# Bidirectional retention: from all 512 x 512 scores to two chunks of 256 tokens with states

## The chip, the cores and the metric

One core of a Trainium2 chip runs the whole program. The metric is device time in microseconds (us): the median of the runs, 1824.52 us before (3 runs, 1824.33 to 1824.80).

## The reference, cut to what matters

Two sequences ("groups") of 512 tokens and 1024 features go through two layers and a final norm. Layer 0 is differential attention, layer 1 is retention in both directions over 8 heads, with 128 features in queries and keys and 256 in values. The change lies in layer 1.

```python
proj = h @ w_in                                # 1024 -> q 1024, k 1024, v 2048, gate 2048
q, k = retention_rotate(q), retention_rotate(k) * 128 ** -0.5
# per head, with decays g_f = exp(log_g_f), g_b = exp(log_g_b); n: query, m: key
# forward:  o_f[n] = sum over m <= n of g_f ** (n - m) * (q[n] . k[m]) * v[m]
# backward: o_b[n] = sum over m >  n of g_b ** (m - n) * (q[n] . k[m]) * v[m]
o = rms_norm(o_f + o_b) * silu(gate)
x = x + o @ w_out
```

The reference takes the sums in chunks of 128 tokens with a state of 128 x 256 carried between them; any other chunk gives the same sums.

## The kernel before, in words

**Numbers in two parts.** Each fp32 operand of a matmul is held as a rounded part (`hi_of`, L469, a cast on ScalarE) and the rest (`lo_of`, L472, a subtraction on VectorE; its instructions stand under L470 and L473). A product takes three passes: hi*hi, hi*lo, lo*hi (`PASSES`, L31).

**Stages.** Projections of layer 0, attention (about 620 to 1000 us), projections of layer 1 (about 1050 to 1500 us), retention with its output projection (1480 us to the end). The projections and the output projections multiply 2 x 2 blocks in seven products (`SEQ`, L44; matmuls L645, L693 and L1384). Rotated queries and keys (`rot_done`, L741), values and gates go to DRAM and come back for the next stage.

**Retention before.** A block is one head and one group: 16 blocks, ordered by pairs of heads (two heads of group 0, the same two of group 1). For a block, `fetch2` (L1549) loads the two parts of q and of k (512 KB each, [128 features, 2, 512 tokens]) and of v (2 x 512 KB), `decay` (L1568) a table of 128 x 896 decays for each head. `score2` (L1572) works on 128 keys and all 512 queries: three matmuls of 512 columns, one multiplication with the table from PSUM on VectorE (L1583), then hi and lo. Four such steps make the block's transposed scores. `av2` (L1589) makes the output of 128 queries: 12 matmuls of 256 columns (4 tiles of keys x 3 passes, L1597). Then the norm (`norm_two` L864, `norm_apply` L885: a square with a sum, a root, a reciprocal, a scaled copy, L868 to L887), two transposes back into the same PSUM bank (`turn_o` L890, matmuls L893), the gate (`gate2` L1318, L1326), sums for the seven products (L1344 to L1358), and `out2` (L1360, L1384), 28 calls of six matmuls of 512 columns for each pair of heads. The weights of a pair are loaded in seven pieces of 512 KB by `w_split` (L1303) into two buffers in turn (`wa`, `wb`) and split by ScalarE and VectorE (1024 columns each). They are due between the last `out2` of one pair and the first of the next.

**The order of the work.** The main loop (L1632 to L1659) walks over 64 tiles (block b, 128 queries t): while tile t of block b is in `av2`, step t of block b+1 is in `score2`, and pieces of `out2` (`fill`) stand between. At t = 3 `fetch2(b + 2)` is called. Nothing is issued there: each call notes operations with a cost, what they read and write, and `Plan.arrange` (L141) simulates the five engines and writes one fixed order for each. PE may be moved by up to 24 operations (`WINDOW`, L75), a load is issued up to 15 us of planned time ahead (`AHEAD`, L79). An engine then takes its list strictly in order and waits at each semaphore.

**Places.** `LATE` (L374) names the buffers of the retention stage; two sets serve even and odd blocks. PSUM: two banks `sc` for scores, two banks `o` for `av2` with its norm and transposes, four for `out2`. The decay tables are made in the projection stage (`decay_table`, L1512: three exponentials a head, L1524 to L1526) and go through DRAM.

## Time and profile before

| what | us |
|---|---|
| median of 3 runs | 1824.52 |
| the profiled execution, own time | 1824.4 |
| its span, first to last instruction | 1822.6 |
| PE (matmuls) busy | 1784.9 (98%) |
| PEld (weight loads, beside PE) busy | 1539.8 (84%) |
| DVE (VectorE) busy | 1477.9 (81%) |
| ACT (ScalarE) busy | 1037.9 (57%) |

The profile is one execution. "Busy" is the time with at least one instruction of that engine under way; since matmuls are pipelined, the time that a matmul costs is read from the distance between starts, not from its own duration. The chain is followed back from the last instruction: each piece is what the next one waited for.

### The profile page before, as it was taken

The numbers are of one execution on the slowest core, as the hardware profiler recorded it, in microseconds if no ns is written. First come the engines' busy times: TensorE is split into PE (matmuls) and PEld (weight loads), VectorE is DVE, ScalarE is ACT, GpSimd is POOL, SyncE is SP. The second block draws the span as 40 slices with busy tenths as digits, with TensorE's granted clock in tenths as the row PEclk, the third lists the DMA queues.
The fourth block names the chain that finished last, engine by engine and source line by source line (L and its number), as shares of the span: only waits on it lengthen the run. The fifth ranks groups of instructions, "written<-read, shape, count | busy, mean of one in ns | idle before, by whom it ended". The sixth has DMA issues, their size and how long they took to land.

```text
span 1822.6 us, 28127 instructions
## 1 busy us (share of the span) xinstructions
PE 1784.9 (98%) x10106; PEld 1539.8 (84%) x10106; DVE 1477.9 (81%) x2599; ACT 1037.9 (57%) x2158; POOL 238.4 (13%) x371
## 2 busy tenths in 40 slices
PE   7999999999999989999999999999999999999998
PEld 6988988988988878888888788989898897888886
DVE  7988888787798799888888898786766858778687
ACT  7644444444444587767767774544453547666564
POOL 3000000000000024343433100000000000111111
PEclk9999999999999999999999999999999999999999
DMA  8467667767766678888786358788775478889784
GB/s 290 164 184 199 201 188 201 207 184 209 197 182 193 229 288 226 238 233 249 230 249 188 135 168 235 233 233 236 228 220 161 151 255 296 247 239 268 221 248 139
DMA packets 197421, 393.85 MB, mean 216 GB/s; under 512 B 16289, under 2 KB 77345, under 8 KB 197153
## 3 DMA queue, kind: packets, MB, share of 16 engines
q1 hardware_dynamic: 174320, 349.76, 57.7%
q0 software_dynamic: 22528, 41.95, 14.3%
q8 instruction: 79, 1.29, 0.3%
q14 instruction: 62, 0.50, 0.1%
q10 hardware_dynamic: 432, 0.34, 0.1%
HBM read 254.10 MB, written 175.64 MB: 236 GB/s over the span
## 4 chain that ended last, share of the span: by engine, by line
PE 82%; DMA 7%; DVE 6%; ACT 2%; issue 2%; POOL 1%; SPq 0%; ACTq 0%; DVEq 0%; POOLq 0%
PE bank L645 39%; PE bank L693 16%; PE bank L1384 12%; PE bank L1267 4%; PE bank L1217 4%; DMA b<-w1P 4%; PE bank L1597 3%; DMA b<-in_da_w_out_dram 1%; PE bank L1579 1%; PE bank L1252 1%; DVE b L473 1%; PE bank L893 1%; DVE arena L473 1%; ACT arena L470 1%; DMA raw<-in_ret_w_in_dram 1%
## 5 line engine op out<-in xcount | busy, mean ns | idle before, releaser
L645 PE MATMUL bank<-arena,ws 128*128 128x512 f32 x2202 | 526.8, 393 | 7.9 <-ACT ws L470 7.0
L645 PEld LDWEIGHTS bank<-arena,ws 128*128 128x128 f32 x2202 | 414.0, 189 | 98.4 <-ACT ws L470 7.0
L645 PE MATMUL bank<-b,ws 128*128 128x512 f32 x1170 | 286.7, 392 | 1.3 <-DVE e L722 1.3
L645 PEld LDWEIGHTS bank<-b,ws 128*128 128x128 f32 x1170 | 219.2, 188 | 48.9 <-DVE e L722 1.4
L1384 PE MATMUL bank<-b,b 128*128 128x512 f32 x794 | 212.3, 399 | 2.8 <-ACT c L1423 1.8
L693 PE MATMUL bank<-ws,arena 128*128 128x256 f32 x1728 | 205.4, 277 | 1.7 <-DVE e L794 1.7
L470 ACT CAST ws<-st 128x512 fp32r<-128x512 f32 (+1 forms) x188 | 129.8, 694 | 132.2 <-PE bank L645 64.0
L693 PEld LDWEIGHTS bank<-ws,arena 128*128 128x128 f32 x1728 | 201.9, 188 | 3.1 <-DVE e L794 1.9
L714 ACT COPY c<-bank 128x512 f32<-128x512 f32 x165 | 96.4, 585 | 166.7 <-PE bank L645 134.1
L473 DVE TENSOR_TENSOR ws<-st,ws 128x512 fp32r<-128x512 f32 (+1 forms) x188 | 144.8, 775 | 50.7 <-ACT ws L470 43.4
L1384 PEld LDWEIGHTS bank<-b,b 128*128 128x128 f32 x794 | 144.8, 189 | 32.9 <-ACT c L1423 2.3
L473 DVE TENSOR_TENSOR b<-b,b 128x512 fp32r<-128x512 f32 (+2 forms) x204 | 137.0, 683 | 22.7 <-ACT b L470 22.4
L470 ACT CAST b<-b 128x512 fp32r<-128x512 f32 (+2 forms) x204 | 123.7, 620 | 44.0 <-DVE b L1583 16.3
L722 DVE TENSOR_TENSOR e<-bank,c 128x512 f32<-128x512 f32 x165 | 113.0, 685 | 40.7 <-PE bank L645 32.1
L473 DVE TENSOR_TENSOR ws<-raw,ws 128x512 fp32r<-128x512 f32 (+1 forms) x143 | 109.5, 773 | 34.7 <-ACT ws L470 20.6
L960 POOL DMA_DIRECT2D x<-b x96 | 85.9, 908 | 365.1 <-DVE b L1428 265.1
L470 ACT CAST ws<-raw 128x512 fp32r<-128x512 f32 (+1 forms) x143 | 99.0, 698 | 51.7 <-PE bank L645 33.0
L693 PE MATMUL bank<-ws,b 128*128 128x256 f32 x960 | 117.7, 277 | 0.0
L693 PEld LDWEIGHTS bank<-ws,b 128*128 128x128 f32 x960 | 114.0, 188 | 0.9
L1233 ACT ACTIVATE b<-bank,nm 128x512 f32<-128x512 f32 x128 | 87.8, 688 | 36.7 <-DVE nm L1225 36.2
L1267 PE MATMUL bank<-arena 128*128 128x256 f32 x768 | 105.7, 287 | 0.2 <-DVE b L1326 0.2
L1217 PE MATMUL bank<-arena 128*128 128x512 f32 x384 | 102.1, 398 | 3.4 <-ACT b L1233 3.4
(190 smaller groups left out, 2812.8 us busy)
## 6 DMA issues: line engine op xcount, KB each, us to landing
qk<-os SPq DMA_DIRECT2D x192, 256.0 KB, 3.9
arena<-qk SPq DMA_DIRECT2D x80, 512.0 KB, 6.2
raw<-in_da_w_in_dram SPq DMA_DIRECT2D x64, 512.0 KB, 5.8
v<-os SPq DMA_DIRECT2D x60, 512.0 KB, 5.3
arena<-v SPq DMA_DIRECT2D x48, 512.0 KB, 5.2
x<-b POOLq DMA_DIRECT2D x96, 256.0 KB, 6.5
raw<-in_ret_w_in_dram SPq DMA_DIRECT2D x48, 512.0 KB, 5.9
g<-e SPq DMA_DIRECT2D x49, 256.0 KB, 5.6
```

The source lines that it names most:

```text
L470: act(n, lambda: nc.scalar.copy(dst(), src()), r, w)
L473: dve(n, lambda: nc.vector.tensor_tensor(dst(), src(), hi().bitcast(F32), op=ALU.subtract), r, w)
L645: nc.tensor.matmul(ps.t, a[u][0]()[:, k, :], bt[k][:, v, :], start=(opens and k == 0 and i == 0), stop=(k == 3 and i == 2), skip_group_che ...
L693: nc.tensor.matmul(ps[:, (t % 2) * 256:(t % 2) * 256 + 256], bt[k][:, v, t * P:(t + 1) * P], a[u][0]()[:, k, :], start=(opens and t % 2 == ...
L714: act(S, lambda c=c, ps=ps: nc.scalar.copy(c.t, ps.t), [ps], [c])
L722: dve(S, lambda e=e, ps=ps, c=c: nc.vector.tensor_tensor(e.t, ps.t, c.t, op=ALU.add), [ps, c], [e])
L960: plan.op("POOL", 1.0, lambda: nc.gpsimd.dma_start(out(), in_(), accum_op=ALU.add), r, w, lands=5.5, kb=kb, hold=hold)
L1217: nc.tensor.matmul(s.t, q[:, u, t * P:(t + 1) * P], k[:, v, :], start=(n == 0), stop=(n == 2))
L1233: act(840, lambda j=j, s=s, m=m: nc.scalar.activation(p[:, j, :], s.t, AF.Exp, bias=m.t, accum_out=sm[:, j:j + 1]), [s, m], [(p, j), (sm, j)])
L1267: nc.tensor.matmul(o[:, 0:256], aT[:, a, j * P:(j + 1) * P], v[b][:, j, :], start=(n == 0), stop=(n == 11))
L1384: nc.tensor.matmul(ps.t, pick(A[i], u), (hi, lo)[v][:, i, :], start=(opens and n == 0), stop=(n == 5), skip_group_check=True)
L1597: nc.tensor.matmul(o[:, 0:256], a_[j][:, u, t * P:(t + 1) * P], v_[v][:, j, :], start=(n == 0), stop=(n == 11))
```

## The change

Retention is computed in two chunks of 256 tokens. Scores are made only inside a chunk (`score2(b, c)`: two tiles of keys x 256 queries, side by side in one bank). Across chunks a state carries the sum: `states` multiplies the transposed, decay-scaled keys of each chunk with its values (128 x 256 for each chunk, one bank), and `av2` adds the decay-scaled queries (`queries`) times the state of the other chunk, which serves forward for chunk 1 and backward for chunk 0. Keys are stored once in fp32 (256 KB a block instead of 512); `keys` splits them on chip, transposes them by TensorE (four transposes into one bank), scales each transposed tile by a column of decays on the way out of PSUM (four copies of 128 columns on ScalarE) and splits the result. The decay tables of a head, 512 KB instead of 448, are one 128 x 512 table for scores, which fits both chunks, one for queries, and four columns for keys. The steps of block b+1 beside tile t of block b are now `keys`, `score2` of chunk 0, `states` with `queries`, `score2` of chunk 1. The fp32 keys have one place for all blocks, and transposed keys and scaled queries share one place in each set. The kernel's other stages keep their code.

```diff
...
-    LATE = dict(q0=["raw0"], k0=["raw1"], v0=["raw2", "raw3"], aT0=["st0", "st1", "st2", "os0"], sg0=["os1"], F0=[3],
-                aT1=[0, 1, 2, "os2"], k1=[4], q1=[5], v1=[6, 7], AB=[8, 9, 10], sg1=[26], F1=[27], wa=[20], wb=[21], S4=[24],
+    LATE = dict(q0=["raw0"], k0=["raw1"], v0=["raw2", "raw3"], aT0=["st0", "st1"], kT0=["st2"], Z0=["os0"], sg0=["os1"], F0=[3],
+                aT1=[0, 1], kT1=[2], Z1=["os2"], k1=[4], q1=[5], v1=[6, 7], AB=[8, 9, 10], sg1=[26], F1=[27], wa=[20], wb=[21], S4=[24],
...
@@ rot_done @@
+            if whole:
+                o = os_t(F32)
+                for n, (p, q, alu) in enumerate(((m1, m2, ALU.subtract), (a, m3, ALU.add))):
+                    dve(S, lambda n=n, p=p, q=q, alu=alu: nc.vector.tensor_tensor(o[:, n, :], p.t, q.t, op=alu),
+                        [p, q], [(o, n)])
+                    for j in range(2):
+                        dma(lambda j=j, n=n: dst[g][j, n * 64:(n + 1) * 64], lambda j=j, n=n: o[j * 64:(j + 1) * 64, n, :],
+                            [(o, n)], [(dst[g], (n, j))], 128)
+                return
...
-    f_d = [dram([P, 896], f"f{h}") for h in range(NH)]
+                        shape = [2, P, S] if layer and which else [2, P, 2, S]
+                        qk_d[layer, which, h, g] = dram(shape, f"qk{layer}{which}{h}{g}")
+    f_d = [dram([P, 2, S], f"f{h}") for h in range(NH)]
     x_d = {(g, t): dram([P, D], f"x{g}{t}") for g in range(NG) for t in range(NT)}
...
@@ decay_table @@
-        act(384, lambda: nc.scalar.activation(a[:, 0:384], a[:, 0:384], AF.Exp, scale=lr[:, 1, h:h + 1]), [lr], [a])
-        act(384, lambda: nc.scalar.activation(b[:, P:S], b[:, P:S], AF.Exp, scale=lr[:, 0, h:h + 1]), [lr], [b])
-        act(P, lambda: nc.scalar.activation(b[:, 0:P], mid.t, AF.Exp), [mid], [b])
-        dma(lambda: f_d[h][:, 0:384], lambda: a[:, 0:384], [a], [(f_d[h], 0)], 192)
-        dma(lambda: f_d[h][:, 384:896], lambda: b.t, [b], [(f_d[h], 1)], 256)
-
+        for n, which in ((0, 1), (3, 0)):
+            at = slice(n * P, n * P + P)
+            act(P, lambda at=at, which=which: nc.scalar.activation(
+                f[:, at], f[:, at], AF.Exp, scale=lr[:, which, h:h + 1]), [lr], [f])
+        for n in (1, 2):
+            act(P, lambda n=n: nc.scalar.activation(f[:, n * P:n * P + P], mid.t, AF.Exp), [mid], [f])
+        for which in range(2):
+            at, half = slice(which * 2, which * 2 + 2), slice((1 - which) * 256, (2 - which) * 256)
+            act(60, lambda at=at, which=which: nc.scalar.activation(
+                dtab[:, h, at], cols[:, at], AF.Exp, scale=lr[:, which, h:h + 1]), [lr, cols], [(dtab, 2 * h + which)])
+            act(256, lambda half=half, which=which: nc.scalar.activation(
+                w[:, half], w[:, half], AF.Exp, scale=lr[:, which, h:h + 1]), [lr], [w])
+        for n, x in enumerate((f, w)):
+            dma(lambda n=n: f_d[h][:, n, :], lambda x=x: x.t, [x], [(f_d[h], n)], 256)
...
@@ fetch2 @@
-        for which in range(2):
-            t = qk[b, which] = late("qk"[which] + str(b % 2), 0, [P, 2, S], F32R)
-            src = qk_d[1, which, h - h % 2, g]
-            dma(lambda t=t: t.t.bitcast(F32), lambda src=src: src[h % 2], [src], [t], 512)
+        q = qk[b, 0] = late("q" + str(b % 2), 0, [P, 2, S], F32R)
+        q_src, k_src = (qk_d[1, which, h - h % 2, g] for which in range(2))
+        kf = kfs[b] = Buf(plan, "kf", 1, lambda i: small[:, 512:1024], lambda i: (-512, 0))
+        dma(lambda: kf.t, lambda: k_src[h % 2], [k_src], [kf], 256)
+        dma(lambda: q.t.bitcast(F32), lambda: q_src[h % 2], [q_src], [q], 512)
...
@@ keys, score2, states, queries, ahead, av2 @@
+    def keys(b):
+        h, kf = blocks[b][0], kfs[b]
+        k = qk[b, 1] = late("k" + str(b % 2), 0, [P, 2, S], F32R)
+        hi_of(S, lambda: k[:, 0, :], lambda: kf.t, [kf], [(k, 0)])
+        lo_of(S, lambda: k[:, 1, :], lambda: kf.t, lambda: k[:, 0, :], [kf, (k, 0)], [(k, 1)])
+        tp = bank("sc", "kT")
+
+        def fn():
+            for j in range(NT):
+                nc.tensor.transpose(tp[:, j * P:(j + 1) * P], kf[:, j * P:(j + 1) * P], ident.t)
+        pe(0.44, fn, [kf, ident], [tp])
+        t = turns("rt", [P, S])
+        for j in range(NT):
+            act(180, lambda j=j: nc.scalar.activation(
+                t[:, j * P:(j + 1) * P], tp[:, j * P:(j + 1) * P], AF.Copy, scale=dtab[:, h, j:j + 1]),
+                [tp, dtab], [(t, j)])
+        kT = kTs[b] = late(f"kT{b % 2}", 0, [P, 2, S], F32R)
+        hi_of(S, lambda: kT[:, 0, :], lambda: t.t, [t], [(kT, 0)])
+        lo_of(S, lambda: kT[:, 1, :], lambda: t.t, lambda: kT[:, 0, :], [t, (kT, 0)], [(kT, 1)])
+
+    def score2(b, c):
         h, g = blocks[b]
         s = bank("sc", "s2")
         q, k = qk[b, 0], qk[b, 1]
 
         def fn():
-            for i, (u, v) in enumerate(PASSES):
-                nc.tensor.matmul(s.t, k[:, u, j * P:(j + 1) * P], q[:, v, :], start=(i == 0), stop=(i == 2))
-        pe(0.69, fn, [q, k], [s])
+            for jj in range(2):
+                j = 2 * c + 1 - jj
+                for i, (u, v) in enumerate(PASSES):
+                    nc.tensor.matmul(s[:, jj * 256:jj * 256 + 256], k[:, u, j * P:(j + 1) * P], q[:, v, c * 256:c * 256 + 256],
+                                     start=(i + jj == 0), stop=(i == 2), skip_group_check=True)
+        pe(0.7, fn, [q, k], [s])
         t1 = turns("rt", [P, S])
         F = Fs[h]
-        dve(S, lambda: nc.vector.tensor_tensor(t1.t, s.t, F[:, 384 - P * j:896 - P * j].bitcast(F32), op=ALU.mult), [s, F], [t1])
-        aT = late(f"aT{b % 2}", j, [P, 2, S], F32R)
+        dve(S, lambda: nc.vector.tensor_tensor(t1.t, s.t, F[:, 0, :].bitcast(F32), op=ALU.mult), [s, F], [t1])
+        aT = late(f"aT{b % 2}", c, [P, 2, S], F32R)
         hi_of(S, lambda: aT[:, 0, :], lambda: t1.t, [t1], [(aT, 0)])
         lo_of(S, lambda: aT[:, 1, :], lambda: t1.t, lambda: aT[:, 0, :], [t1, (aT, 0)], [(aT, 1)])
-        aTs[b, j] = aT
+        aTs[b, c] = aT
+
+    def states(b):
+        z = bank("sc", "z2")
+        kT, v_ = kTs[b], vt[b]
+
+        def fn():
+            for c in range(2):
+                n = 0
+                for u, v in PASSES:
+                    for j in (2 * c, 2 * c + 1):
+                        nc.tensor.matmul(z[:, c * 256:c * 256 + 256], kT[:, u, j * P:(j + 1) * P], v_[v][:, j, :],
+                                         start=(c + n == 0), stop=(n == 5), skip_group_check=True)
+                        n += 1
+        pe(1.4, fn, [kT, *v_], [z])
+        Z = Zs[b] = late(f"Z{b % 2}", 0, [P, 2, S], F32R)
+        hi_of(S, lambda: Z[:, 0, :], lambda: z.t, [z], [(Z, 0)])
+        lo_of(S, lambda: Z[:, 1, :], lambda: z.t, lambda: Z[:, 0, :], [z, (Z, 0)], [(Z, 1)])
+
+    def queries(b):
+        F, q, t = Fs[blocks[b][0]], qk[b, 0], turns("rt", [P, S])
+        dve(S, lambda: nc.vector.tensor_tensor(
+            t.t, q[:, 0, :].bitcast(F32), q[:, 1, :].bitcast(F32), op=ALU.add), [q], [t])
+        dve(S, lambda: nc.vector.tensor_tensor(t.t, t.t, F[:, 1, :].bitcast(F32), op=ALU.mult), [t, F], [t])
+        w = qw[b] = late(f"kT{b % 2}", 0, [P, 2, S], F32R)
+        hi_of(S, lambda: w[:, 0, :], lambda: t.t, [t], [(w, 0)])
+        lo_of(S, lambda: w[:, 1, :], lambda: t.t, lambda: w[:, 0, :], [t, (w, 0)], [(w, 1)])
+
+    def ahead(b, n):
+        if n == 0:
+            keys(b)
+        elif n == 2:
+            states(b)
+            queries(b)
+        else:
+            score2(b, n // 2)
 
     def av2(b, t):
         o = bank("o")
-        a_, v_ = [aTs[b, j] for j in range(NT)], vt[b]
+        c = t // 2
+        aT, v_, q, Z = aTs[b, c], vt[b], qw[b], Zs[b]
 
         def fn():
             n = 0
             for u, v in PASSES:
-                for j in range(NT):
-                    nc.tensor.matmul(o[:, 0:256], a_[j][:, u, t * P:(t + 1) * P], v_[v][:, j, :],
-                                     start=(n == 0), stop=(n == 11))
+                for jj in range(2):
+                    at = jj * 256 + t % 2 * P
+                    nc.tensor.matmul(o[:, 0:256], aT[:, u, at:at + P], v_[v][:, 2 * c + 1 - jj, :],
+                                     start=(n == 0), stop=False)
                     n += 1
-        pe(1.37, fn, [*a_, *v_], [(o, 0)])
+            for i, (u, v) in enumerate(PASSES):
+                nc.tensor.matmul(o[:, 0:256], q[:, u, t * P:(t + 1) * P], Z[:, v, (1 - c) * 256:(2 - c) * 256],
+                                 start=False, stop=(i == 2))
+        pe(1.06, fn, [aT, *v_, q, Z], [(o, 0)])
...
-    fetch2(1)
...
-    for j in range(NT):
-        score2(0, j)
+    for n in range(4):
+        ahead(0, n)
+        if n == 0:
+            fetch2(1)
...
-                score2(b + 1, t)
+                ahead(b + 1, t)
...
@@ _tables @@
-    dist = np.arange(896, dtype=np.float32)[None, :] - 384.0 - np.arange(P, dtype=np.float32)[:, None]
+    p, c = np.arange(P, dtype=np.float32)[:, None], np.arange(S, dtype=np.float32)[None, :]
+    dist = c - p - np.float32(P) * np.array([1, 1, 2, 2], dtype=np.float32).repeat(P)[None, :]
+    cols = np.concatenate([255 - p, 127 - p, -p, -128 - p], axis=1)
+    rows = (c - np.float32(S // 2) + (c >= S // 2)) + 0 * p
...
```

## Rows read from the trace of the kernel before

**Rows 1.** The page: busy time of each engine over the span.

```profile
PE 1784.9 (98%) x10106; PEld 1539.8 (84%) x10106; DVE 1477.9 (81%) x2599; ACT 1037.9 (57%) x2158; POOL 238.4 (13%) x371
```

**Rows 2.** Busy time in three stretches: attention, second projections, retention. Columns stand on the first line.

```profile
core 0: us, PE busy (x) PEld busy (x) DVE busy (x) ACT busy (x) POOL busy (x), PEclk, DMA share, GB/s
700.00:860.00 160.00, 160.00 (x941) 138.23 (x940) 139.44 (x285) 114.77 (x289) 65.08 (x109) 1.00 0.83 240
1050.00:1350.00 300.00, 298.04 (x1681) 259.43 (x1680) 238.05 (x374) 153.16 (x260) 14.79 (x15) 1.00 0.77 227
1500.00:1800.00 300.00, 291.86 (x1669) 248.81 (x1668) 231.06 (x475) 196.32 (x486) 46.02 (x56) 0.99 0.84 246
```

**Rows 3.** Chain that ended last, in time: start us, us, engine, tile, line, count.

```profile
1051.20 93.66 PE bank L645 x408
1153.07 27.23 PE bank L693 x240
...
1621.88 0.22 PE bank L893 x2
1622.10 0.69 PE bank L1579 x3
1622.79 1.38 PE bank L1384 x6
1624.17 1.41 PE bank L1597 x12
```

**Rows 4.** Groups of instructions, 1505 to 1796 us; the last over the span.

```profile
L1583 DVE TENSOR_TENSOR b<-bank,b 128x512 f32<-128x512 f32 x29 | 19.4, 677 | 2.5 <-PE bank L1579 2.5
L473 DVE TENSOR_TENSOR b<-b,b 128x512 fp32r<-128x512 f32 x66 | 44.6, 685 | 8.4 <-ACT b L470 8.2
L470 ACT CAST b<-b 128x512 fp32r<-128x512 f32 x66 | 40.0, 616 | 13.6 <-DVE b L1583 13.3
L887 ACT ACTIVATE small<-bank,crr 128x256 f32<-128x256 f32 x62 | 29.3, 473 | 15.1 <-DVE crr L871 15.1
...
L1526 ACT ACTIVATE e<-small 128x128 f32<-128x128 f32 x8 | 2.5, 307 | 1.6 <-DVE small L1523 1.6
```

**Rows 5.** The same chain at the four places where it leaves the matmuls.

```profile
1504.52 0.04 DVE b L1583
...
1533.05 1.69 PE bank L1597 x12
...
1581.40 0.43 DVE b L1326
...
1585.98 5.95 DMA b<-w1P
...
1597.96 10.22 DMA b<-w1P
...
1613.70 1.70 PE bank L1597 x12
...
1660.26 0.43 DVE b L1326
...
1691.80 2.62 PE bank L1384 x6
...
1741.28 0.44 DVE b L1326
...
1773.66 1.70 PE bank L1597 x12
```

**Rows 6.** Busy time in slices of 20 us, columns as in rows 2.

```profile
1500.00:1520.00 20.00, 18.45 (x116) 15.01 (x115) 18.24 (x39) 13.24 (x35) 0.00 (x0) 1.00 1.01 374
...
1680.00:1700.00 20.00, 17.63 (x90) 14.64 (x89) 13.22 (x27) 11.35 (x27) 2.60 (x3) 0.91 0.78 222
...
1740.00:1760.00 20.00, 20.00 (x117) 17.39 (x116) 18.05 (x34) 15.07 (x36) 4.35 (x5) 1.00 0.95 242
```

**Rows 7.** Who PE waited for, 1480 us to the end: total, times, longest.

```profile
PE bank L1384 <- ACT c L1423: 1.8, 2, 1.4
```

More of the change, by code (lines that the diff above doesn't have):

```diff
@@ L738, in evac, with rot_done @@
                 self.done(1, 0, X, s, True)
-    def rot_done(dst, tab, scaled):
+    def rot_done(dst, tab, scaled, whole=False):
         def mul(out, a, tab_, psum):
@@ L949, in trunk_kernel @@
                     if layer == 0 or h % 2 == 0:
-                        qk_d[layer, which, h, g] = dram([2, P, 2, S], f"qk{layer}{which}{h}{g}")
-    f_d = [dram([P, 896], f"f{h}") for h in range(NH)]
+                        shape = [2, P, S] if layer and which else [2, P, 2, S]
+                        qk_d[layer, which, h, g] = dram(shape, f"qk{layer}{which}{h}{g}")
+    f_d = [dram([P, 2, S], f"f{h}") for h in range(NH)]
     x_d = {(g, t): dram([P, D], f"x{g}{t}") for g in range(NG) for t in range(NT)}
@@ L1010, in units2 @@
         ropes = [Unit(w2, which * D + h * P, "pair",
-                      rot_done({g: qk_d[1, which, h, g] for g in range(NG)}, tab2, which == 1), parity_view)
+                      rot_done({g: qk_d[1, which, h, g] for g in range(NG)}, tab2, which == 1, which == 1), parity_view)
                  for h in range(0, NH, 2) for which in range(2)]
```

23 lines of the change are left out of this document (12 added, 11 removed).

## The prediction

> **What bounds the kernel now.** First the page: PE is busy 98% of the span, its weight loads 84%, VectorE 81%, ScalarE 57% [rows 1]. Then busy time by stretch: in attention PE has no gap, in the second projections it is busy 298 of 300 us, and from 1500 to 1800 us, where retention runs, 291.9 of 300; in that stretch VectorE is at 231 us, ScalarE at 196, and the DMA engines at a share of 0.84 [rows 2]. So PE is the bound, retention is the stage with most idle PE (8.1 us), and what the other engines can still take there is 69 us (VectorE) and 104 us (ScalarE). Last the chain, which tells more than the averages: through most of the kernel it runs from matmul group to matmul group [rows 3], but in retention it leaves PE four times. At 1504.5, 1581.4, 1660.3 and 1741.3 us it goes over to VectorE, from there to a load of output weights (w1P, two in each place; the pair at 1585.98 and 1597.96 takes 5.95 and 10.22 us), through the split on ScalarE and VectorE to the release of a bank, and comes back to PE at 1533.1, 1613.7, 1691.8 and 1773.7 us [rows 5]. These four stretches last 28.5, 32.3, 31.5 and 32.4 us, 124.7 us of the 300. They are where a pair of heads ends and the seven weight pieces of the next are loaded and split. In them PE isn't the bound: it is nearly full, but waits at the end. A measurement of this kernel can tell a difference of about 0.2%, 3.6 us, from none.
>
> **PE, block by block.** In the chain three matmuls of 512 columns of a score cost 0.69 us, 12 of 256 columns of the output 1.41 us (0.1175 each), two transposes 0.22 us [rows 3]. A block before is 4 x 0.69 + 4 x 1.41 = 8.40 us. After, it has 12 matmuls of 256 columns for scores (1.41), 12 for states (1.41), 4 x 9 for outputs (4.23) and four transposes (0.44): 7.49 us. That is 0.91 us less, and 16 blocks give **14.6 us** less PE work. The price of the 256-column matmul is the one thing to choose: the projections have it at 27.23 / 240 = 0.1135 us [rows 3], which on the 24 new ones of a block would give 1.5 us more over 16 blocks; I take 0.1175, since retention's own groups are as short.
>
> **A page's rule against it.** The weight loads do not go down: 60 in a block before, 64 after. In the rows a load with 512 columns behind it costs 93.66 / 408 = 0.230 us and one with 256 costs 0.1135 us [rows 3], so columns and not loads set the pace of the 512-column groups. The Trainium skill (Perfetto Trace Analysis, Identifying the Most-Contended Engine) says that matmul busy time is a poor measure and that the busy share of weight loads should be used instead. By that reading PE is bound by loads; it is a rival below, and the trace speaks against it with the two numbers of this paragraph.
>
> **What of the 14.6 us lies on the path.** Where PE leads, all of it. In the four stretches the chain is loads and splits, whose length does not depend on the matmuls, so there a shorter matmul list only makes PE wait longer at the end. Their share is 124.7 / 300 = 0.416, so 6.1 us of the 14.6 is lost there and 8.5 us stays.
>
> **What is added on VectorE and ScalarE.** VectorE does 8 operations of 512 columns a block before (four table multiplications, four rests) and 10 after (keys two rests, scores two multiplications and two rests, states one rest, queries a sum, a multiplication and a rest). At 0.68 us [rows 4] that is +1.37 us a block, 22 us in all. ScalarE does four casts of 0.616 us before; after it does six and four scaled copies of 128 columns out of PSUM. Such a copy isn't in the trace: it lies between 0.307 us (128 columns without a scale column) and 0.473 us (256 columns with one) [rows 4]; I take 0.37, a little under the middle. That gives +2.7 us a block (2.5 to 3.1), 43 us in all. With 22 and 43 us more the stage has VectorE at 253 and ScalarE at 239 us of less than 300. Attention runs without a gap in PE with VectorE at 139.4 of 160 us (87%) [rows 2], so where PE leads I cost this at nothing; its cover is PE's own list of up to 24 operations ahead. But the four stretches are fuller: VectorE is at 18.2 of 20 us in the first and 18.1 in the last [rows 6]. A stretch of 31 us holds 31 / 18.75 = 1.66 blocks, so 2.3 us more VectorE work. Nothing of it to all of it can land on the chain; about half of a stretch's chain is loads, so I take half, 1.15 us, four times: **+4.6 us** (0 to 9.2).
>
> **What is taken off the DMA engines.** Keys come as 256 KB instead of 512, the table of a head as 512 instead of 448 KB: about 0.23 MB less a block, at 246 GB/s [rows 2] 0.9 us of DMA time, 1.5 us a stretch. The loads on the chain take 5.95 and 10.22 us for the same 512 KB [rows 5], so they share the engines with others. If all the relief lands on them it is 6 us over four stretches, if none, 0: I take half, **-3.0 us**.
>
> **Costed at nothing.** Projections: the keys' 16 casts and 16 rests and half of the keys' stores go, and the decay tables take eight exponentials a head instead of three (at no more than 0.473 us each, under 31 us for all). ScalarE is busy 153 and VectorE 238 of 300 us there while PE has 298 [rows 2], so neither the relief nor the load reaches PE; if that cover were gone, a wait of one exponential at each of 8 heads is 4 us. SP's queue has as many issues as before. The keys' load now waits until `keys` of the block before has let go of their one place; behind it on SP's queue stand q, v, gate and w1P loads. The place is let go three tiles (some 14 us) before the load is needed, and a load lands in 6 to 10 us [rows 5], so it is covered; if not, one tail of 4 us at the start, where blocks 0 and 1 follow each other closely. The longer row of steps before the first output (split, transpose, scale, split, state) stands beside the last projections; the state and queries of a block are made two tiles before they are used.
>
> **Sum.** -14.6 + 6.1 + 4.6 - 3.0 = -6.9 us. Made against the profiled execution's own 1824.4 us, that is 1817.5; the median of the runs is 0.1 us above that execution, so it stands for both.
>
> **Rivals.**
> 1. **The saving comes through in full.** The order is written anew, loads may go up to 15 us ahead, and the stretches shrink with the rest: -14.6, 1809.8 us. For it: PE is idle only 8.1 us of 300 [rows 2], so the stretches have little slack either way. Against: the chain's loads wait for their two buffers, not for matmuls. 23%.
> 2. **VectorE fills the stretches.** All 2.3 us land on each of four chains and the loads gain nothing: -14.6 + 6.1 + 9.2 = +0.7 us; with half of the DMA relief, -2.3 us. No change that can be told: about 1823.5 us. For it: 18.2 and 18.1 of 20 us [rows 6]. Against: 13.2 of 20 in the third. 16%.
> 3. **Slower: the clock falls at the end of every stretch.** In the third one PE waits for ScalarE, the longest such wait being 1.4 us [rows 7]; the granted clock of that slice is 0.91 [rows 6], so part of it ran at the lower of the two levels (1.2 of 2.4 GHz), and the six matmuls after the wait take 2.62 us [rows 5] against 1.38 [rows 3], with 12 of the output behind them slow too, some 1.8 us together. If the added casts make the wait as long at the other three ends, on top of rival 2, it is +0.7 + 3 x 1.8 = +6.1, 1830.5 us. It decides from waits like the third stretch's at most ends. 7%.
> 4. **Weight loads are the bound** (the rule above): four more a block at 0.1175 us, 16 blocks, +7.5 us, 1831.9 us. 2%.
>
> **How the numbers follow.** The forecast has 52%: 1817.5 us, with its own bounds from -14.6 + 6.1 - 6 (1809.9) to rival 2's 1823.5. Rival 1 lies at the low bound. The range, 1809.5 to 1823.5, leaves out rivals 3 and 4 and what of rival 1 goes below it through shorter 256-column matmuls. Faster by over 0.2% (under 1820.9): forecast and rival 1, 75%. Within 0.2%: rival 2, 16%. Slower: rivals 3 and 4, 9%.
>
> **What the profile after would show.** Right: PE's busy time down by 14 to 15 us; in the chain 0.70 us for six score matmuls, 1.41 for twelve of states, about 1.06 for nine of outputs; VectorE at some 85% and ScalarE at some 80% of the retention stage; four stretches around w1P loads, each about as long as now, with PE idle of 3 to 4 us in each. Wrong: a chain that stays on PE through the stretches (rival 1), a wait for the keys' load or for the four scaled copies, PE idle spread over all tiles, or slices at a lower clock at three or four ends (rival 3).

## The result, and the profile after

The changed kernel takes 1833.46 us (median of 8 runs, 1829.2 to 1837.17) against 1824.42 us before (8 runs, 1819.89 to 1828.49): ratio 1.0049, 95% interval 1.0032 to 1.0067. It is slower by 9 us, where 6.9 us faster was forecast. Executions of one kernel lie some 5 us on either side of their median, and the profiled one of the changed kernel is a short one (own time 1829.8, span 1828.0), so its trace shows 5.4 us of the 9. Its mean granted clock, 0.999, is also the highest of the eight (their mean is 0.997), so what the clock costs in the others doesn't show in it.

The page of the changed kernel, busy time of each engine (to [rows 1]):

```profile
PE 1778.1 (97%) x10170; PEld 1532.2 (84%) x10170; DVE 1485.2 (81%) x2615; ACT 1064.2 (58%) x2278; POOL 240.6 (13%) x371
```

PE has 6.8 us less to do and takes 5.4 us longer: its idle time rose from 1822.6 - 1784.9 = 37.7 to 1828.0 - 1778.1 = 49.9 us. So waits of 12 us came. The busy time fell by less than the 14 to 15 us that the prediction named as its sign of being right; 4.1 us of what is missing is a group of projection matmuls that became slower (L645 below).

Busy time in two stretches, columns on the first line (to [rows 2]):

```profile
core 0: us, PE busy (x) PEld busy (x) DVE busy (x) ACT busy (x) POOL busy (x), PEclk, DMA share, GB/s
1050.00:1350.00 300.00, 297.82 (x1655) 257.14 (x1654) 230.84 (x361) 150.30 (x270) 14.78 (x15) 1.00 0.73 218
1500.00:1800.00 300.00, 281.43 (x1744) 244.01 (x1743) 244.11 (x501) 224.07 (x576) 44.98 (x54) 1.00 0.84 240
```

Two things are to be seen. In retention PE is idle 18.6 of 300 us instead of 8.1, although VectorE and ScalarE are far from full. And in the projections, whose matmuls the change leaves alone, 1655 of them stand in the same 300 us where 1681 stood before: they run late.

The chain that ended last, at the prices of the new matmul groups and around one of its new pieces (to [rows 3, 5]; start us, us, engine, tile, line, count; "..." marks pieces left out):

```profile
1576.04 0.72 PE bank L1623 x6
...
1578.14 0.71 PE bank L1679 x6
1578.85 0.36 PE bank L1683 x3
...
1605.38 10.02 DMA b<-w1P
...
1622.27 0.45 PE bank L1603 x4
...
1622.77 8.72 DMA small<-qk
1631.52 0.63 ACT arena L470
...
1632.17 0.58 DVE arena L473
...
1634.66 0.35 DVE b L1336
1635.01 0.04 issue
1635.05 0.98 PE bank L1679 x6
```

L1623 are scores, L1679 and L1683 the two parts of an output, L1603 the transposes of the keys. `small<-qk` is the load of the whole keys into their one place; the kernel before has no such piece. From 1581 to 1749 us the chain holds seven of them, 6.89 to 10.60 us long. Each ends at ScalarE's cast of the next block's keys. Five start where the four transposes of one block let go of the place, two some 0.5 us later, behind other loads that the queue was issuing.

What that does to ScalarE and VectorE, from their own lists in time, with the transposes back on PE that the gate needs (start us, us, engine, line, operation, count; in brackets what the engine waited before it):

```profile
1627.27 0.41 ACT L470 CAST b<-b 128x256 fp32r<-128x256 f32 x1
1631.52 0.62 ACT L470 CAST arena<-small 128x512 fp32r<-128x512 f32 x1 [3.84 <-DMA small<-qk]
1632.04 1.14 ACT L470 CAST b<-b 128x512 fp32r<-128x512 f32 x2
1633.08 0.37 ACT L877 ACTIVATE bank<-bank 128x256 f32<-128x256 f32 x1
```

```profile
1631.17 0.38 PE L902 MATMUL bank<-ident,small 128*128 128x128 f32 x2
```

```profile
1629.22 0.42 DVE L473 TENSOR_TENSOR b<-b,b 128x256 fp32r<-128x256 f32 x1
1632.17 0.69 DVE L473 TENSOR_TENSOR arena<-small,arena 128x512 fp32r<-128x512 f32 x1 [2.53 <-ACT arena L470]
...
1634.58 0.42 DVE L1336 TENSOR_TENSOR b<-bank,b 128x256 f32<-128x256 f32 x1
```

ScalarE stands still for 3.84 us in front of the cast, with the square of a norm (L877), which needs nothing of the keys, behind it in its list. VectorE stands still too, for 2.53 us in front of the keys' rest (L473), which needs the cast; behind it stand four other operations and then a gate (L1336). The transposes that this gate needs had started at 1631.17, so it is held by its place in VectorE's list and not by its operands. The gate frees the bank, and PE's output group at 1635.05 had waited 0.66 us for that bank. In four of the seven pieces the chain goes on by the rest of the keys on VectorE, in the other three by what stands behind the cast on ScalarE.

The waits of PE, first the same one in the kernel before (other line numbers), and under them those of ScalarE, from 1480 us to the end (to [rows 7]; total, times, longest):

```profile
PE bank L1597 <- DVE b L1326: 2.7, 5, 1.1
```

```profile
PE bank L1679 <- DVE b L1336: 8.5, 13, 1.4
PE bank L1394 <- ACT c L1433: 3.4, 2, 2.2
PE bank L1643 <- DMA arena<-v: 3.2, 4, 1.5
```

```profile
ACT arena L470 <- DMA small<-qk: 18.1, 7, 3.8
ACT b L470 <- DMA small<-qk: 12.2, 5, 5.2
ACT b L470 <- DMA b<-w1P: 8.1, 4, 2.9
```

ScalarE waits 30.3 us for the keys, in 12 places. PE waits 8.5 us for banks that the gate frees (2.7 before) and, what never happened before, 3.2 us for values: these are the states' matmuls (L1643). All its waits in this stretch come to 21.3 us, against 8.0 before.

Groups of instructions in the changed kernel, the first over the span, the second from 1505 to 1796 us; then the load issues over the span (KB, median us from issue to landing):

```profile
L645 PE MATMUL bank<-b,ws 128*128 128x512 f32 x1170 | 290.8, 395 | 1.5 <-DVE e L722 1.5
...
L1607 ACT ACTIVATE b<-bank,dtab 128x128 f32<-128x128 f32 x56 | 17.0, 364 | 5.0 <-PE bank L1603 5.0
```

```profile
small<-qk SPq DMA_DIRECT2D x16, 256.0 KB, 7.2
```

The same L645 group had 286.7 us and 392 ns before:

```profile
L645 PE MATMUL bank<-b,ws 128*128 128x512 f32 x1170 | 286.7, 392 | 1.3 <-DVE e L722 1.3
```

Of these 1170 matmuls 690 stand in the projections of layer 0 and 480 in those of layer 1. With that the projections end some 5 us later (last L693 at 1504.6 instead of 1499.2 us), and retention, from there to the end, takes 323.4 us in both profiled executions: all that it saved on PE it lost in waits.

### The profile page after: what moved, and what is told of

It is laid out like the page before. It is cut to its first block, busy times and chain, and to the rows that moved or that the text cites. A ratio compares the mean times of both kernels' runs of the same rounds, so it can differ in the third digit from the quotient of the medians.

```text
span 1828.0 us, 28378 instructions
## 1 busy us (share of the span) xinstructions
PE 1778.1 (97%) x10170; PEld 1532.2 (84%) x10170; DVE 1485.2 (81%) x2615; ACT 1064.2 (58%) x2278; POOL 240.6 (13%) x371
## 3 DMA queue, kind: packets, MB, share of 16 engines
q0 software_dynamic: 22528, 41.95, 14.4%
## 5 line engine op out<-in xcount | busy, mean ns | idle before, releaser
L645 PE MATMUL bank<-arena,ws 128*128 128x512 f32 x2202 | 527.2, 393 | 8.7 <-ACT ws L470 8.0
L645 PEld LDWEIGHTS bank<-arena,ws 128*128 128x128 f32 x2202 | 413.6, 189 | 100.6 <-ACT ws L470 8.0
L645 PE MATMUL bank<-b,ws 128*128 128x512 f32 x1170 | 290.8, 395 | 1.5 <-DVE e L722 1.5
L645 PEld LDWEIGHTS bank<-b,ws 128*128 128x128 f32 x1170 | 219.2, 188 | 52.7 <-DVE e L722 2.1
L693 PE MATMUL bank<-ws,arena 128*128 128x256 f32 x1728 | 205.0, 277 | 1.7 <-DVE e L803 1.7
L693 PEld LDWEIGHTS bank<-ws,arena 128*128 128x128 f32 x1728 | 201.4, 188 | 3.2 <-DVE e L803 1.9
L473 DVE TENSOR_TENSOR ws<-st,ws 128x512 fp32r<-128x512 f32 (+1 forms) x188 | 145.4, 779 | 64.2 <-ACT ws L470 57.1
L473 DVE TENSOR_TENSOR b<-b,b 128x512 fp32r<-128x512 f32 (+2 forms) x196 | 132.0, 686 | 19.0 <-ACT b L470 19.0
L473 DVE TENSOR_TENSOR ws<-raw,ws 128x512 fp32r<-128x512 f32 (+1 forms) x143 | 109.8, 779 | 41.0 <-ACT ws L470 16.6
L470 ACT CAST b<-b 128x512 fp32r<-128x512 f32 (+2 forms) x196 | 119.3, 621 | 24.6 <-DMA b<-w1P 8.1
L693 PE MATMUL bank<-ws,b 128*128 128x256 f32 x960 | 118.8, 278 | 0.9 <-DVE e L722 0.9
L693 PEld LDWEIGHTS bank<-ws,b 128*128 128x128 f32 x960 | 114.7, 188 | 1.7 <-DVE e L722 1.1
```

Of the source, the lines that this page charges most:

```text
L470: act(n, lambda: nc.scalar.copy(dst(), src()), r, w)
L473: dve(n, lambda: nc.vector.tensor_tensor(dst(), src(), hi().bitcast(F32), op=ALU.subtract), r, w)
L645: nc.tensor.matmul(ps.t, a[u][0]()[:, k, :], bt[k][:, v, :], start=(opens and k == 0 and i == 0), stop=(k == 3 and i == 2), skip_group_che ...
L693: nc.tensor.matmul(ps[:, (t % 2) * 256:(t % 2) * 256 + 256], bt[k][:, v, t * P:(t + 1) * P], a[u][0]()[:, k, :], start=(opens and t % 2 == ...
```

## The experiments

Three theories came out of these rows. **P, placing:** the table `dtab` (32 columns, 128 bytes in each partition) is placed between the buffers `b` and the weight buffers `ws`; the distance between the two, as the built programs place them, grew from 131,520 to 131,648 bytes, and matmuls with one operand in `b` and one in `ws` became slower. **W, the cast of the keys stands too early:** the planner counts on a landing time of 2.0 + KB/200 us, 3.3 us for this load, and puts the cast that soon after the release of the place; the load takes 7.2 us, and ScalarE waits at the head of its list. **V, the values:** `states` for block b+1 run beside tile 2 of block b, while the outputs, which alone needed the values before, come two tiles later. Against them stood **S** (the four stretches of the prediction, in which a shorter list of matmuls buys nothing) and **L** (the amount of work on VectorE and ScalarE).

| kernel | median us | ratio to before, 95% interval | mean granted clock |
|---|---|---|---|
| changed | 1833.46 | 1.0049 (1.0032 to 1.0067) | 0.9970 |
| P undone | 1827.69 | 1.0025 (1.0008 to 1.0042) | 0.9968 |
| W undone | 1827.23 | 1.0033 (1.0016 to 1.0051) | 0.9958 |
| P, W undone | 1822.31 | 0.9991 (0.9977 to 1.0005) | 0.9958 |
| P, V undone | 1819.66 | 0.9993 (0.9978 to 1.0009) | 0.9961 |
| W, V undone | 1821.40 | 0.9992 (0.9978 to 1.0005) | 0.9953 |
| P, W, V undone | 1813.71 | 0.9943 (0.9921 to 0.9965) | 0.9962 |
| before, 128 bytes more | 1826.92 | 1.0015 (1.0001 to 1.0029) | 0.9983 |
| P undone, keys in two parts ("two parts") | 1820.37 | 0.9970 (0.9952 to 0.9989) | 0.9962 |
| two parts, V undone | 1821.35 | 0.9991 (0.9979 to 1.0003) | 0.9961 |
| two parts, w1P casts late | 1830.05 | 1.0028 (1.0009 to 1.0048) | 0.9939 |
| two parts, less scaling | 1820.22 | 0.9986 (0.9970 to 1.0002) | 0.9958 |
| before, one set of weights | 1814.95 | 0.9953 (0.9935 to 0.9970) | 0.9978 |
| two parts, one set | 1811.69 | 0.9929 (0.9909 to 0.9948) | 0.9963 |

The kernels ran in groups, each group beside the kernel before on one chip, so between groups it is the ratios that are compared. They are not the quotients of the medians, which differ from them by up to 1.3 thousandths (0.9950 for the kernel with all three undone). Every edit but that of the distance lets the planner write a new order, so what an edit is worth includes all that it moves. The granted clock is the mean over a kernel's runs; the kernel before has 0.9978 to 0.9982 in the four groups beside it.

**1. The table out of the way.** One more column than needed, so that the table falls among the small buffers and the distance is as before (its uses change with it):

```diff
-    cols, dtab = const([P, 4], "cols"), const([P, NH, 4], "dtab")
+    cols, dtab = const([P, 4], "cols"), const([P, 33], "dtab")
```

> The changed kernel with the 128 bytes of key decays moved to the pool of small columns, so that the distance between the b buffers and the ws buffers is that of before. Theory P (placing: the 128 new bytes change that distance, and projection matmuls that read b and ws pay for it): the matmuls of line 645 on b and ws go back from 395 to 392 ns mean, the last one of them starts near 1461 us instead of 1465, and the time is 4 to 5 us under the changed kernel, about +4 us (ratio 1.002) to before. Rival (the late projections are chance of one profile): no difference to the changed kernel, ratio 1.005.

Measured 1827.69, ratio 1.0025. The group that had 395 ns is back:

```profile
L645 PE MATMUL bank<-b,ws 128*128 128x512 f32 x1170 | 286.6, 391 | 0.0
```

**2. The counter-proof on the kernel before**, with 32 columns of padding at the same place:

```diff
+    pad = const([P, 32], "pad")
+    dve(8, lambda: nc.vector.tensor_scalar(pad[:, 0:8], lr[:, 0, :], -1.0, None, op0=ALU.mult), [lr], [pad])
```

> The kernel before with one more column buffer of 128 bytes a partition at the place where the change put its key decays, written by one VectorE operation of 8 columns and read by nobody; order and work as before. Theory P: 4 to 5 us slower than before, and the matmuls of line 645 on b and ws at 395 instead of 392 ns. Rival: within 1 us of before.

Measured 1826.92, ratio 1.0015, and the group turns as slow as in the changed kernel:

```profile
L645 PE MATMUL bank<-b,ws 128*128 128x512 f32 x1170 | 290.7, 395 | 0.0
```

The time rose by 1.5 thousandths, 2.7 us, less than the 4 to 5 us expected, though these lie inside the interval. P holds, in both directions: 1170 matmuls take 4 us longer for 128 bytes between buffers. How PE comes to feel the distance, no run shows.

**3. The late cast.** Upon experiment 1, the planner is told a landing time for this one load, in place of its 2.0 + KB/200 us:

```diff
-        dma(lambda: kf.t, lambda: k_src[h % 2], [k_src], [kf], 256)
+        dma(lambda: kf.t, lambda: k_src[h % 2], [k_src], [kf], 256, lands=8.0)
```

> As e1, and the planner is told that the load of the whole keys takes 8 us to land (it assumes 3.3; the profile after shows a median of 7.3), so it puts the cast that waits for it later in ScalarE's list. Theory W (the cast stands too early in an in-order list, and what is behind it, the norm and the release of the output banks, is late): ScalarE's waits on that load fall from 30 us to under 8, PE's wait for the release of output banks from 8.5 to about 4 us, and the time is 6 to 10 us under e1, so 2 to 6 us under before. Theory L (the 22 us of VectorE and 43 us of ScalarE work that were added use up the matmuls' gain): those waits move elsewhere and the time stays within 2 us of e1.

Measured 1822.31, ratio 0.9991. ScalarE's wait for the keys, 32.2 us in experiment 1 (17.8 + 14.4), is down to this:

```profile
ACT arena L470 <- DMA small<-qk: 1.8, 2, 1.3
```

W holds: 3.4 thousandths, 6 us, come from the place of one cast in ScalarE's list, with the order that follows from it; the load itself is no faster. PE's wait for banks that the gate frees fell from 7.9 to 4.5 us, but its wait for norms (L902 for L896) rose from 0.6 to 7.0. What also shows is the clock. PE in the first stretch of this kernel, columns as above:

```profile
1500.00:1505.00 5.00, 4.82 (x41) 4.61 (x39) 1.93 (x4) 1.53 (x4) 0.00 (x0) 1.00 1.02 369
1505.00:1510.00 5.00, 2.16 (x14) 1.72 (x15) 4.87 (x11) 5.00 (x18) 0.00 (x0) 0.97 1.04 365
1510.00:1515.00 5.00, 4.41 (x21) 4.01 (x21) 3.27 (x7) 3.40 (x8) 0.00 (x0) 0.50 0.87 306
1515.00:1520.00 5.00, 4.41 (x21) 4.01 (x20) 4.81 (x13) 4.32 (x12) 0.00 (x0) 0.50 0.77 260
```

After 5 us in which PE was busy 2.16, it ran 10 us at 1.2 of 2.4 GHz, 8.8 us of them busy, so at most some 4.4 us of work was lost. The changed kernel's profiled execution shows a clock of 1.00 in every such slice up to 1820 us. Over all runs the mean granted clock fell from 0.9968 in experiment 1 to 0.9958 here.

**4. Keys in two parts**, stored and loaded as before (512 KB, two places); the whole keys for the transposes are a sum on VectorE:

```diff
-        hi_of(S, lambda: k[:, 0, :], lambda: kf.t, [kf], [(k, 0)])
-        lo_of(S, lambda: k[:, 1, :], lambda: kf.t, lambda: k[:, 0, :], [kf, (k, 0)], [(k, 1)])
+        dve(S, lambda: nc.vector.tensor_tensor(
+            kf.t, k[:, 0, :].bitcast(F32), k[:, 1, :].bitcast(F32), op=ALU.add), [k], [kf])
```

> As e1, with the keys stored and loaded in two parts as before (512 KB, no cast and no rest on chip); the whole keys for the transposes are made by one sum on VectorE, so VectorE has as many operations as the changed kernel and ScalarE one cast less a block. Theory W: no cast waits for a load, time 6 to 10 us under e1. Theory L: within 3 us of e1 (one ScalarE cast a block less is 10 us of its 224).

Measured 1820.37, ratio 0.9970: faster than before. As the change has it, keeping the keys whole saves bytes and costs time. The page, of an execution that took 1811.4 us, 9 below the median:

```profile
PE 1769.5 (98%) x10170; PEld 1534.3 (85%) x10170; DVE 1493.3 (83%) x2631; ACT 1066.4 (59%) x2278; POOL 240.7 (13%) x371
```

PE is 15.4 us under the kernel before here, about the forecast 14.6; of that, this kernel gains 5.4 by its ratio (0.0030 x 1824) and 3.1 by the medians of its group.

**5, 6. Without the stretches.** Is the rest lost where pairs of heads end (theory S)? In both kernels only the first pair's output weights are loaded and split, and all pairs use them, so the output projection of three pairs is not that of the reference:

```diff
-                if (g, r) == (1, 1):
+                if (g, r) == (1, 1) and not layer:
```

> The kernel before, with the retention output weights of the first pair of heads used for all four pairs: the 21 later loads and splits of weight pieces (w_split) are left out, so the output projection of three pairs is not computed with its own weights. All matmuls stay. Theory S (the four stretches around these loads are off PE's path): PE idle from 1500 to 1800 us falls from 8 to 3 us or less and the time is 5 to 10 us under before. Theory L (VectorE and ScalarE work is what counts): the same sign, since 21 x 1.2 us of VectorE work go too. This run is the base of the next one.

> The chunked kernel with keys in two parts (e4), with the same loads and splits left out as in the run before. Theory S: without the stretches the matmuls' saving comes through, so this is 11 to 15 us under the run before, against 3 us (median) to 5 us (ratio) between e4 and the kernel before. Theory L (the added VectorE and ScalarE work takes it): 3 to 6 us under the run before, as with the stretches.

Measured 1814.95 (ratio 0.9953) and 1811.69 (0.9929). Between them lie 3.3 us by the medians, 4.4 by the ratios; the change is worth no more without the stretches than with them (5.4 in experiment 4). The two profiled executions are 8.2 us apart in span (1813.5 and 1805.3), so single executions would have told another tale. S falls as the main cause: the forecast for it was 11 to 15 us, and 4.4 us is known to some 5.

**7. The same remedy for the output weights.** Upon experiment 4, the loads of w1P are planned with 9 us:

```diff
-                dma(lambda: t.t, lambda: src, [src], [t], 512)
+                dma(lambda: t.t, lambda: src, [src], [t], 512, lands=9.0 if layer else None)
```

> e4, and the planner is told that the weight pieces of retention take 9 us to land instead of 4.6 (its casts wait for them 5 to 15 us in the profiles). Theory S with the same cause as for the keys (casts too early in ScalarE's list): ScalarE's wait on w1P nearly gone, 2 to 5 us under e4. If the stretches are set by the loads themselves: within 2 us of e4, or slower, since the pieces come later in the plan.

Measured 1830.05, ratio 1.0028: slower than experiment 4 by 10 us, a miss. ScalarE no longer waits for w1P, but the whole order has shifted, and PE waits for values instead; the mean granted clock, 0.9939, is also the lowest of all:

```profile
PE bank L1643 <- DMA arena<-v: 12.2, 7, 2.1
```

**8. Less scaling.** Upon experiment 4, one plain copy out of PSUM for the four scaled ones, and one operation less in `queries`; the decays of the keys and the rest of the queries are left out:

```diff
-        for j in range(NT):
-            act(180, lambda j=j: nc.scalar.activation(
-                t[:, j * P:(j + 1) * P], tp[:, j * P:(j + 1) * P], AF.Copy, scale=dtab[:, 4 * h + j:4 * h + j + 1]),
-                [tp, dtab], [(t, j)])
+        act(S, lambda: nc.scalar.copy(t.t, tp.t), [tp], [t])
```

> e4 with the decays of the keys left out (one plain copy of 512 columns in place of four scaled ones of 128) and the queries scaled from their rounded part alone (one VectorE operation less): 0.9 us of ScalarE and 0.68 us of VectorE work less a block, 14 and 11 us in all. The keys' decays and the rest of the queries are not computed. Theory L: at least 4 us under e4. Theory S: within 2 us of e4, since where PE leads these engines have room.

Measured 1820.22, ratio 0.9986, no gain over 0.9970, where L had at least 4 us. So L finds no support: less work on VectorE and ScalarE bought nothing here, though the order moved as well, and the wait for values with it (3.1 us in experiment 4):

```profile
PE bank L1640 <- DMA arena<-v: 7.9, 5, 2.5
```

That row stood at 0 in the kernel before and at 1.4 to 12.2 us in all the kernels above with states. It led to V.

**9, 10. States a step later**, first with keys in two parts (upon 4), then with whole keys and the late cast (upon 3):

```diff
-        elif n == 2:
+        elif n == 3:
             states(b)
             queries(b)
         else:
-            score2(b, n // 2)
+            score2(b, n - 1)
```

> Keys in two parts and the buffers' distance as before; the steps of a block ahead are keys, scores of chunk 0, scores of chunk 1, then states with queries, so that the states need the values a tile later than in the changed kernel. Theory V (what is still missing of the 14.6 us goes partly to the states' waits for the values, 3.1 us in the kernel with keys in two parts, 5.2 us with keys whole): the wait of the states' matmuls for the values falls under 0.5 us and the time is 2 to 5 us under the two-part kernel's 1820.4 (ratio to before 0.994 to 0.996). Theory L (the longer row of steps is what counts): state and scaled queries are then ready a tile before their first use instead of two, so PE waits for them at L1683 by 0.2 to 0.5 us a block, and the time is 3 to 8 us above (ratio 0.999 to 1.001). Rival: the waits move on to the bank of the outputs and nothing changes within 0.15%.

> Keys whole as in the changed kernel, distance of the buffers as before, the planner told that the keys' load takes 8 us, and the states with the queries a step later. Theory V: 2 to 5 us under the 1822.3 of the kernel with the late cast alone (ratio to before 0.996 to 0.998), the states' wait for the values (1.7 us there) gone. Theory L: 3 to 8 us above, PE waiting for the scaled queries or the state at L1683. Rival: no change within 0.15%.

The first measured 1821.35, ratio 0.9991: no gain over 0.9970, a miss for V, though the wait for values is gone from its trace. The second measured 1813.71, ratio 0.9943: 4.8 thousandths better than the late cast alone (8.8 us, where 2 to 5 were expected), and the fastest of the kernels that leave nothing out. Its waits of PE, and its retention stage:

```profile
PE bank L902 <- ACT small L896: 6.1, 3, 3.0
PE bank L1679 <- DVE b L1336: 5.1, 8, 1.2
```

```profile
1500.00:1800.00 300.00, 288.63 (x1795) 254.96 (x1795) 253.82 (x519) 228.25 (x582) 46.12 (x56) 0.99 0.84 244
```

1795 matmuls stand in the 300 us in which the changed kernel has 1744. This execution has a disturbance of its own: the projections' group L693 (2688 matmuls) stands at a mean of 279 ns here and in experiment 3, against 276 to 278 in the other kernels with whole keys and in the kernel before, though the buffers stand as in experiment 1. No run shows why.

**11 to 13. Do the three add up?** V with the cast early, W alone, and W with V, the latter two with the changed kernel's own distance. The edits are those above.

> The changed kernel with the buffers' distance as before and the states with the queries a step later; the cast of the whole keys stands as early as in the changed kernel. Beside it in this call: the late cast alone, and late cast with later states. With the ratios to before so far (changed 1.0049, distance undone 1.0025, with the late cast 0.9991, with later states too 0.9943) theory V, three causes that add up, forecasts 1.0025 - 0.0048 = 0.998, some 1819 us. Theory W alone (the early cast holds ScalarE's list, and what the states wait for does not matter as long as it does): 1.0025, 1828 us, with 25 to 35 us of ScalarE's waits for the keys' load as in the changed kernel.

> The changed kernel with one edit: the planner told that the keys' load takes 8 us. Three causes that add up: 1.0049 - 0.0034 = 1.0015, some 1826.5 us; the projections' matmuls stay slow (395 ns, 2.79 us for twelve). If the late cast alone were the whole of the loss, 0.997 to 0.999, 1818 to 1822 us.

> The changed kernel with the late cast and the later states, but with its own distance between the buffers (128 bytes more than before). Three causes that add up: the kernel with all three undone had 0.9943, the distance costs 0.0015 (measured on the kernel before) to 0.0024 (on the changed one), so 0.9958 to 0.9967, 1815 to 1818 us. If the 0.9943 of that kernel was a lucky hand of six runs and later states are worth nothing: 1.0015, as the late cast alone.

Measured 0.9993, 1.0033 and 0.9992. Later states thus gain in all three pairs with whole keys: 1.0025 to 0.9993, 1.0033 to 0.9992, 0.9991 to 0.9943, that is 3.2, 4.1 and 4.8 thousandths (6 to 9 us). The distance costs 2.4, 4.2 and 4.9, the early cast 1.6, 3.4 and 5.0 thousandths, each read from the three pairs that differ in it alone; on the kernel before the distance cost 1.5. "Adds up" holds within what these runs can tell (each ratio is known to 1.2 to 2.2 thousandths), but all three forecasts by adding up came out too low: P with V by 1.3 thousandths, W alone by 1.8, and W with V by 2.5 above the upper end of its forecast, which had taken the distance at the lower prices. So the 0.9943, from six runs, may be in part a lucky hand, and with it the highest price of each cause. Of the nine pairs two stood side by side in one group: the late cast upon P undone (3.4) and later states upon W undone (4.1). Along one path the three undo 1.0049 - 0.9943 = 10.6 thousandths, 19 us.

By which way V helps is only partly shown. With the late cast, PE's wait for values was 1.4 us (W alone) and 1.7 us (P, W undone), less than the 7 to 9 us gained. The loads of the keys, in the kernel with P and W undone and then with later states too (load issues, 1500 to 1800 us):

```profile
small<-qk SPq DMA_DIRECT2D x13, 256.0 KB, 8.3
```

```profile
small<-qk SPq DMA_DIRECT2D x13, 256.0 KB, 5.4
```

Why they land sooner, the queue's issues around 1655 us suggest, again in the one and the other:

```profile
1653.72 0.80 SPq L464 DMA_DIRECT2D b<-v  x2
1654.57 0.43 SPq L464 DMA_DIRECT2D arena<-qk  x1
1656.14 0.32 SPq L464 DMA_DIRECT2D small<-qk  x1
```

```profile
1653.58 0.81 SPq L464 DMA_DIRECT2D b<-v  x2
1655.98 0.32 SPq L464 DMA_DIRECT2D small<-qk  x1
1656.34 0.49 SPq L464 DMA_DIRECT2D arena<-qk  x1
```

With the states later, the 512 KB of queries (`arena<-qk`) go behind the keys instead of in front of them, and the keys land in 5.4 instead of 8.1 us. The 1 MB of values stays in front of the keys here, as at most places; it moves behind them at three of thirteen (at 1540, 1616 and 1694 us), and at others it is issued 2.4 us ahead of the keys instead of 1.0. In the median they land 3 us sooner with the later states in this pair, 2.8 in the one with the changed kernel's own distance (8.1 and 5.3), and 2.2 in the pair with the cast early (7.9 and 5.7); there ScalarE's wait for the keys falls from 32.2 to 8.6 us by this edit alone:

```profile
ACT arena L470 <- DMA small<-qk: 8.6, 6, 2.3
```

So in that pair V works at least in part through W, beside the wait for values, which falls from 5.2 us to none. In the other two the way stays open: the granted clock of two profiled executions points at itself (in slices of 20 us, P and W undone ran at 0.74 in the first and 0.91 in the last stretch; with V undone too, the one slice of retention before 1800 us below 1.00 is that from 1680 us, at 0.91), but over all runs its mean hardly moves (0.9958 to 0.9962, and 0.9958 to 0.9953).

## Why the prediction was wrong, step by step

**What bounds the kernel: right.** PE was the bound and still is; its idle time is what the change added to. The four numbered rivals don't describe the result either: 1833.46 us lies near the 1830.5 of rival 3 and the 1831.9 of rival 4, but by chance, as their mechanisms (below) are not what the runs show.

**PE, block by block: right in kind, a little too much.** A block was to go from 8.40 to 7.49 us. The chain has 0.71 or 0.72 for scores (1.41 forecast for two), 1.44 for states (1.41), 0.71 + 0.36 for an output (1.06) and 0.45 for the transposes (0.44): 1.43 + 1.44 + 4.28 + 0.45 = 7.60. That is 0.80 x 16 = 12.8 us instead of 14.6.

**Rival 4, the weight loads: fell.** Groups of 256 columns cost what the row before said, at four loads more a block. The Trainium skill (Perfetto Trace Analysis, Identifying the Most-Contended Engine) judges how close TensorE is to its peak by the busy share of weight loads, together with the share of peak arithmetic, and not by matmul busy time; that loads set the pace is the prediction's own reading of it. Here that share is 84% before and after, while the time moved by 9 us one way and, in experiment 10, 10 us the other at 85%, so it told nothing of this change.

**"What is added on VectorE and ScalarE": sizes right, term unneeded.** The scaled copy, taken at 0.37 us, has 364 ns. VectorE was to reach 253 us of 300; it has 253.8 in experiment 10, where PE is held up less, and ScalarE 228 (239 forecast). Experiment 8 took part of that work away and gained nothing, so nothing speaks for the +4.6 us of this step as a cost, nor for rival 2.

**"What is taken off the DMA engines": no relief.** The share is 0.84 before and after, and the chain's w1P loads take 10.02, 9.68 and 10.52 us. The -3.0 us were not there.

**"What of the 14.6 us lies on the path": not the place of the loss.** Without the stretches the change with keys in two parts is worth 3 to 4 us (experiments 5 and 6), with them 3 to 5 (experiment 4). The saving wasn't lost in four places, but in waits that stand at nearly every block.

**"Costed at nothing": here it failed, in three of its sentences.**

The keys' load: "The place is let go three tiles (some 14 us) before the load is needed ... so it is covered". I read that off the loop. But the order that runs is the planner's, and it sets the cast by its own landing time of 3.3 us: in the chain the place falls free at 1622.7 us, the cast stands before work of ScalarE from 1627.7 us on, and the load lands at 1631.5. The landing times that I had (6 to 10 us [rows 5]) were the right ones; I held them against the wrong distance. I also asked only what waits for the load, not what stands behind the cast on ScalarE and behind the rest on VectorE: norms and gates of other tiles. The price is 3.4 thousandths in experiment 3, 1.6 to 5.0 over the pairs.

The projections: "neither the relief nor the load reaches PE". That holds, but a table of 128 bytes moved the buffers, and PE's own matmuls got slower there, a cost that isn't in any list of operations. It is 1.5 to 4.9 thousandths; 4 us (2.2 thousandths) stand directly in the rows of L645.

"The state and queries of a block are made two tiles before they are used" looks at what is made and not at what it needs: the values, 1 MB a block, are wanted two tiles sooner than before, and PE waits 3.2 us for them; with the states later the keys land sooner as well. Moving the states a step later gains 3.2 to 4.8 thousandths with whole keys.

**Rival 3, the clock: not the main cause of this result, but real.** In the profiled execution of the slower kernel the clock is at 1.00 in retention up to 1820 us, so its 5.4 us come without it. Over all eight runs the mean granted clock is 0.9970, against 0.9978 to 0.9982 in the kernel before (in the later groups): a shortfall of 0.001, which I estimate at some 2 of the 9 us (0.001 x 1824, if PE was busy in all of it). In experiment 3 the clock falls in the first stretch and costs up to 4.4 us there, more than the 1.8 that the rival gave for one. Every kernel with the change has a mean of 0.9970 or less; the kernel before and its two variants have 0.9978 or more.

With the three causes out, the change gives 0.9943, 10.4 us (6.4 to 14.4) of the 12.8 on PE: 1813.71, inside the range that was given for the change itself; as a test of the forecast that is luck, since it is another order. What keeps back the rest, some 2 us, is inside that interval; the clock, 0.9962 against 0.9978 in its group, would by the same estimate be 2.9 us. Why later states gain nothing with keys in two parts stays open.

## What to carry to other kernels

When a load gets a single place, read how long it takes from release to landing and compare that with where the planner will put the first user, not with where the loop has it; then look at what else stands behind that user on its engine, and behind what that user feeds on the next engine. When a step is moved ahead, ask for each operand when it must now be there. And a constant that is added anywhere moves buffers: compare the mean of untouched groups before and after first, and put the bytes back to be sure: a mean can also move with the buffers in place, as L693's did in experiment 10.

## What was not expected of the hardware

The pace of matmuls depends on where operands lie in SBUF: 1170 matmuls of 512 columns went from 391 or 392 to 395 ns (286.6 to 290.7 us) with the distance between two groups of buffers 131,648 instead of 131,520 bytes, in the changed kernel and in the kernel before alike, while the 2202 of the same line with operands in other buffers (`arena` and `ws`), whose distance stays as it was, kept to 393 or 394. Traces of four kernels with the greater distance have 395, those of the others 391 to 393.

Half the bytes did not make a load quicker: the keys' 256 KB took 7.2 us in the median, the values' 512 KB 4.9 and 5.5 in the same kernel. What stood ahead of it in the queue counted for more (5.3 to 5.7 us with the states later).
